# Two of the three sums of a woven weight slice, moved from VectorE to GpSimd

## The chip, the cores and the metric

The kernel runs on one core of a Trainium2 chip. The metric is the device time of one execution in microseconds (us). Before the change it is 2104.18 us, the median of 3 runs that lie between 2104.1 and 2104.22 us.

## The reference, cut to what matters

A two-layer decoder trunk over 256 tokens with 2048 columns, all in float32: layer 0 mixes by attention with a forget gate, layer 1 by dilated windows, and each mixer is followed by the same MLP, whose hidden width is 8192.

```
def sq_relu_mlp(h, w_up, w_down):
    a = jax.nn.relu(h @ w_up)
    return (a * a) @ w_down
...
    for i in range(DEPTH):
        ...
        x = x + mix.astype(x.dtype)
        h = rms_norm(x, mlp_norm_g[i])
        x = x + sq_relu_mlp(h, mlp_w_up[i], mlp_w_down[i]).astype(x.dtype)
```

The change touches only the product `h @ w_up` of the two MLPs, and of that only the part that is computed with seven half-size products.

## The kernel before, in words

**Weights in units.** All weights stream from HBM once, through five buffers `raw` of 128 x 2 x 512 floats. TensorE multiplies in a rounded float32 format, so each unit of weights is split in two: ScalarE copies the rounded part to `wh` (L376), and VectorE writes the rest, raw minus rounded, to `wl` (L382). There are five buffers each of `wh` and `wl`. A product needs three matmuls: rounded with rounded (L437), rounded with rest (L438), rest with rounded (L439). The split of a unit is issued when TensorE has used up the unit five places ahead of it, so at most four units lie ready ahead of TensorE.

**Plain units.** One plain unit feeds 12 matmuls of 512 columns, issued by `product_steps`.

**Woven slices.** Of each MLP's up-projection, 80 slices (10 column blocks, 8 slices each; 160 in the kernel) are computed with seven products of half the size in place of eight. They are woven between plain units of other products, at places that the tables `FIRST_BETWEEN`, `BETWEEN` and `LAST_BETWEEN` list; mostly one slice follows one plain unit. A slice takes up two units: the **quarters** unit, three quarters of the raw weights as they are (ScalarE's cast L370, VectorE's rest L374, both 768 wide), and the **sums** unit, four sums and differences of the raw quarters that are kept in a tile `quarters` (cast L376 from `quarters`, rest L382 from `quarters`). TensorE reads them in L1073 to L1077: nine matmuls on the quarters unit, twelve on the sums unit.

**The sums.** `sum_quarters` makes the sums in three instructions on VectorE: L394 (two differences at once, 512 columns), then L398 (256 columns, the tile's part `c`, from a raw quarter and a part that L394 wrote) and L400 (256 columns, `d`, from a raw quarter and `c`). It is a generator, so that the three stand at different places: L394 ahead of the plain unit's L382, L398 behind it, L400 ahead of the quarters unit's L374. There is one buffer `quarters`, shared with other work.

**What sets the order.** Each engine carries out its instructions in the order in which they were written; the function `pin` fixes that order. Small jobs of the MLP stand between the units: the seven products are combined by L1040 to L1048, which read PSUM, turned by L1005, and split by L1025 (ScalarE) and L1027 (VectorE).

**GpSimd.** Before the change it does little: 20 fills of a quarter with zeros (L368, at a block's first slice), a few powers (L598, L626), and it issues the 96 transfers that add a result to `x` in memory (L945), four at a time.

Of the kernel before, what the change touches and what calls it, by code (L numbers as in the profile page):

```python
# [21 lines left out]
NC = 512  # L22
# [21 lines left out]
HC = NC // 2  # L44
# [61 lines left out]
def trunk(ctx: ExitStack, tc, x, fox_w_in, fox_b_f, fox_q_gain, fox_k_gain, fox_w_out, dil_w_in,  # L106
          dil_q_gain, dil_k_gain, dil_w_out, mix_norm_g, mlp_norm_g, mlp_w_up, mlp_w_down, out):
    nc = tc.nc
# [250 lines left out]
    def split_part(i, part):  # L359
        nonlocal summing  # L360
        n, of = units[i]
        raw, (hi, lo) = raws[n], splits[i]
        if of == "sums":
            raw = quarters.pop()
        if "quarters" in of:

            if of == "first quarters":
                nc.gpsimd.memset(hi[:, 1, HC:NC].bitcast(F32), 0.0)  # L368
            flat_hi, flat_lo, flat = (x.rearrange("p k n -> p (k n)")[:, 0:3 * HC] for x in (hi, lo, raw))
            nc.scalar.copy(flat_hi, flat)  # L370
            for _ in summing or sum_quarters(n):
                pass
            summing = None
            nc.vector.tensor_sub(flat_lo, flat, flat_hi.bitcast(F32))  # L374
            return
        nc.scalar.copy(hi[:, part, :], raw[:, part, :])  # L376

        coming = i + 1 < len(units) and "quarters" in units[i + 1][1]
        if coming:
            summing = sum_quarters(units[i + 1][0])  # L380
            next(summing)
        nc.vector.tensor_sub(lo[:, part, :], raw[:, part, :], hi[:, part, :].bitcast(F32))  # L382
        if coming:
            next(summing)
# [3 lines left out]
    def sum_quarters(n):  # L388


        raw = raws[n]
        t = work.tile([P, 2, NC], F32, tag="sd", name=f"quarters{n}", bufs=1)
        neg, c, d = t[:, 0, HC:NC], t[:, 1, 0:HC], t[:, 1, HC:NC]
        nc.vector.tensor_sub(t[:, 0, :].rearrange("p (q n) -> p q n", q=2),  # L394
                             raw.rearrange("p k n -> p (k n)")[:, HC:3 * HC].rearrange("p (q n) -> p q n", q=2),
                             raw[:, 1, HC:NC].unsqueeze(1).to_broadcast([P, 2, HC]))
        yield
        nc.vector.tensor_add(c, raw[:, 0, HC:NC], neg)  # L398
        yield
        nc.vector.tensor_sub(d, raw[:, 0, 0:HC], c)  # L400
        quarters.append(t)

    def next_load():
# [842 lines left out]
```

## Time and profile before

| what | value |
|---|---|
| median of 3 runs | 2104.18 us (2104.1 to 2104.22) |
| span of the profiled execution | 2099.8 us |
| time outside the span (2104.18 less 2099.8) | 4.4 us |
| busy: TensorE matmul, VectorE, ScalarE, GpSimd | 2094.2, 1775.9, 1299.5, 141.3 us |
| granted TensorE clock | 1.00 throughout |
| woven stretches | 440 to 925 us and 1523 to 2022 us of the span |

The profile gives the span of one execution, from its first to its last instruction; its time as the runs measure it isn't given apart, so the 4.4 us between the span and the median are carried along unchanged. In the profile PE is TensorE, DVE VectorE, ACT ScalarE, POOL GpSimd, SP the queue that issues most DMAs. A row of the timeline has the start, the duration, the engine, the line, the operation, the tile written and those read, the shape, and in brackets the idle time before it with what ended it. A row of a group has the busy time, the mean of one in ns, and the idle time ahead. A row of the waits has the total, the number of times and the longest.

### The profile page before, as it was taken

To read this page: it belongs to the slowest core of one execution; us is meant where nothing else is said; L and a number is where in the kernel's file an instruction comes from. 1 tells how busy PE (TensorE), PEld (TensorE's weight loads), DVE (VectorE), ACT (ScalarE), POOL (GpSimd) and SP (SyncE) were. 2 spreads that over 40 slices of the span, in tenths; PEclk is the share of its full clock that TensorE was granted. 3 is DMA by queue.
4 is the path that set the end of the run, shared out by engine and by line. 5 is a ranking of instruction groups with operands and counts; after the bars stand their busy time and mean duration, and the time that the engine had idled before them with its cause. 6 is when DMAs were issued, how large, how long until landed. Compare 5 with 4: busy or idle time off the path is not lost.

```text
span 2099.8 us, 32579 instructions
## 1 busy us (share of the span) xinstructions
PE 2094.2 (100%) x11515; PEld 1881.5 (90%) x11515; DVE 1775.9 (85%) x2613; ACT 1299.5 (62%) x1895; POOL 141.3 (7%) x162
## 2 busy tenths in 40 slices
PE   9999999999999999999999999999999999999999
PEld 7888888899999999998888888888899999999998
DVE  6888876989999999998768787767899989999974
ACT  6565654766666666664655665646656766666663
POOL 2000000001100100110010010000001101001000
PEclk9999999999999999999999999999999999999999
DMA  8888877887888877887877776867878878788884
GB/s 258 254 264 262 259 248 222 272 261 241 252 243 249 262 240 252 258 249 236 280 239 230 247 242 211 269 202 243 277 231 261 241 250 248 231 251 256 265 262 152
DMA packets 375010, 518.28 MB, mean 247 GB/s; under 512 B 43112, under 2 KB 176576, under 8 KB 374848
## 3 DMA queue, kind: packets, MB, share of 16 engines
q1 hardware_dynamic: 360608, 503.23, 75.4%
q0 software_dynamic: 13824, 12.59, 4.0%
q8 instruction: 90, 1.47, 0.3%
q14 instruction: 72, 0.59, 0.1%
q10 hardware_dynamic: 416, 0.39, 0.1%
HBM read 463.12 MB, written 40.39 MB: 240 GB/s over the span
## 4 chain that ended last, share of the span: by engine, by line
PE 100%; DVE 0%; ACT 0%; issue 0%
PE acc L437 26%; PE acc L438 26%; PE acc L439 26%; PE halves_n L1077 6%; PE halves_n L1076 6%; PE halves_n L1075 6%; PE halves_n L1073 1%; PE sc_d L749 0%; PE sc_f L749 0%; PE po_f L698 0%; PE po_d L698 0%; PE sc_d L746 0%; PE acc L486 0%; PE acc L485 0%; PE acc L487 0%; PE pf L760 0%
## 5 line engine op out<-in xcount | busy, mean ns | idle before, releaser
L382 DVE TENSOR_TENSOR wl<-raw,wh 128x1024 fp32r<-128x1024 f32 (+1 forms) x643 | 775.6, 1214 | 228.0 <-ACT wh L376 217.9
L376 ACT CAST wh<-raw 128x1024 fp32r<-128x1024 f32 (+1 forms) x643 | 664.9, 1043 | 403.7 <-PE acc L439 323.7
L437 PE MATMUL acc<-wh,hT_n 128*128 128x512 f32 x1280 | 486.5, 380 | 0.4 <-ACT hT_n L580 0.3
L438 PE MATMUL acc<-wl,hT_n 128*128 128x512 f32 x1280 | 485.4, 379 | 0.0
L439 PE MATMUL acc<-wh,hT_n 128*128 128x512 f32 x1280 | 485.3, 379 | 0.0
L376 ACT CAST wh<-quarters 128x1024 fp32r<-128x1024 f32 x160 | 168.0, 1050 | 260.8 <-DVE quarters L400 243.4
L439 PEld LDWEIGHTS acc<-wh,hT_n 128*128 128x128 f32 x1280 | 241.9, 189 | 34.6 <-DVE hT_n L581 0.4
L437 PEld LDWEIGHTS acc<-wh,hT_n 128*128 128x128 f32 x1280 | 242.1, 189 | 33.2 <-ACT hT_n L580 1.0
L438 PEld LDWEIGHTS acc<-wl,hT_n 128*128 128x128 f32 x1280 | 242.2, 189 | 32.6 <-DVE wl L382 0.5
L382 DVE TENSOR_TENSOR wl<-quarters,wh 128x1024 fp32r<-128x1024 f32 x160 | 195.1, 1219 | 43.0 <-ACT wh L376 43.0
L437 PE MATMUL acc<-wh,aTh_n1a 128*128 128x512 f32 x512 | 194.3, 379 | 0.0
L438 PE MATMUL acc<-wl,aTh_n1a 128*128 128x512 f32 x512 | 194.0, 379 | 0.0
L439 PE MATMUL acc<-wh,aTl_n1a 128*128 128x512 f32 x512 | 194.0, 379 | 0.0
L438 PE MATMUL acc<-wl,aTh_n3a 128*128 128x512 f32 x480 | 182.2, 380 | 0.0
L437 PE MATMUL acc<-wh,aTh_n3a 128*128 128x512 f32 x480 | 182.1, 379 | 0.0
L439 PE MATMUL acc<-wh,aTl_n3a 128*128 128x512 f32 x480 | 181.9, 379 | 0.0
L1077 PE MATMUL halves_n<-wh,sums_n 128*128 128x256 f32 x640 | 176.0, 275 | 0.0
L1076 PE MATMUL halves_n<-wl,sums_n 128*128 128x256 f32 x640 | 176.0, 275 | 0.0
L1075 PE MATMUL halves_n<-wh,sums_n 128*128 128x256 f32 x620 | 170.5, 275 | 0.0
L374 DVE TENSOR_TENSOR wl<-raw,wh 128x768 fp32r<-128x768 f32 x160 | 152.3, 952 | 0.0
L370 ACT CAST wh<-raw 128x768 fp32r<-128x768 f32 x160 | 133.1, 832 | 28.9 <-PE acc L439 15.1
L1077 PE MATMUL halves_n<-wh,hT_n 128*128 128x256 f32 x480 | 132.0, 275 | 0.0
(660 smaller groups left out, 3499.1 us busy)
## 6 DMA issues: line engine op xcount, KB each, us to landing
raw<-in_mlp_w_up_dram SPq DMA_DIRECT2D x256, 512.0 KB, 5.1
raw<-in_mlp_w_down_dram SPq DMA_DIRECT2D x256, 512.0 KB, 4.9
raw<-in_dil_w_in_dram SPq DMA_DIRECT2D x192, 256.0 KB, 3.5
raw<-in_fox_w_in_dram SPq DMA_DIRECT2D x94, 512.0 KB, 4.8
raw<-in_fox_w_out_dram SPq DMA_DIRECT2D x32, 512.0 KB, 4.9
raw<-in_dil_w_in_dram SPq DMA_DIRECT2D x32, 512.0 KB, 4.4
raw<-in_dil_w_out_dram SPq DMA_DIRECT2D x32, 512.0 KB, 3.6
x<-y_n POOLq DMA_DIRECT2D x96, 128.0 KB, 6.0
```

The source lines that it names most:

```text
L370: nc.scalar.copy(flat_hi, flat)
L374: nc.vector.tensor_sub(flat_lo, flat, flat_hi.bitcast(F32))
L376: nc.scalar.copy(hi[:, part, :], raw[:, part, :])
L382: nc.vector.tensor_sub(lo[:, part, :], raw[:, part, :], hi[:, part, :].bitcast(F32))
L437: nc.tensor.matmul(acc[t], ah[:, tok], hi, start=first, stop=False)
L438: nc.tensor.matmul(acc[t], ah[:, tok], lo, start=False, stop=False)
L439: nc.tensor.matmul(acc[t], al[:, tok], hi, start=False, stop=last)
L1073: nc.tensor.matmul(banks[bank], ah, wide.rearrange("p b (h n) -> p b n h", h=2), start=True, stop=False)
L1075: nc.tensor.matmul(to, ah, hi, start=pr == 0 and i == 3, stop=False)
L1076: nc.tensor.matmul(to, ah, lo, start=False, stop=False)
L1077: nc.tensor.matmul(to, al, hi, start=False, stop=pr == KC // 2 - 1 and i > 2)
```

## The change

The two additions of 256 columns are issued on GpSimd. L394 stays on VectorE.

```
         yield
-        nc.vector.tensor_add(c, raw[:, 0, HC:NC], neg)
+        nc.gpsimd.tensor_add(c, raw[:, 0, HC:NC], neg)
         yield
-        nc.vector.tensor_sub(d, raw[:, 0, 0:HC], c)
+        nc.gpsimd.tensor_sub(d, raw[:, 0, 0:HC], c)
         quarters.append(t)
```

On VectorE, in a run of slices of the first MLP (the number behind a tile's name tells the tiles of one name apart; a row has line, operation, tile written, tiles read, shape):

```order
 L394 TENSOR_TENSOR quarters_4782<-raw_4670 128x512
 L382 TENSOR_TENSOR wl_4780<-raw_4640,wh_4779 128x1024
-L398 TENSOR_TENSOR quarters_4782<-raw_4670,quarters_4782 128x256
-L400 TENSOR_TENSOR quarters_4782<-raw_4670,quarters_4782 128x256
 L374 TENSOR_TENSOR wl_4801<-raw_4670,wh_4800 128x768
 L382 TENSOR_TENSOR wl_4818<-quarters_4782,wh_4817 128x1024
 L394 TENSOR_TENSOR quarters_4835<-raw_4731 128x512
```

The quarters unit's L374 now follows the plain unit's L382 directly, and nothing on VectorE stands between L374 and the sums unit's L382 in such a slice.

On GpSimd, a little further on in the same MLP, around one group of transfers and one fill:

```order
+L398 TENSOR_TENSOR quarters_5496<-raw_5380,quarters_5496 128x256
+L400 TENSOR_TENSOR quarters_5496<-raw_5380,quarters_5496 128x256
+L398 TENSOR_TENSOR quarters_5600<-raw_5535,quarters_5600 128x256
 L368 MEMSET wh_5618 128x256
+L400 TENSOR_TENSOR quarters_5600<-raw_5535,quarters_5600 128x256
```

The pairs stand in GpSimd's queue in the order of the slices; a block's first slice has the fill between its two additions.

And on GpSimd at the slice whose `quarters` tile has number 5823:

```order
+L398 TENSOR_TENSOR quarters_5823<-raw_5724,quarters_5823 128x256
 L945 DMA x_103<-y_n_2_0_0_220_5829 128x256
 L945 DMA x_103<-y_n_2_0_1_220_5832 128x256
 L945 DMA x_103<-y_n_2_1_0_220_5843 128x256
 L945 DMA x_103<-y_n_2_1_1_220_5846 128x256
+L400 TENSOR_TENSOR quarters_5823<-raw_5724,quarters_5823 128x256
```

Here four transfers stand between the slice's two additions; this is so at 4 of the 160 slices. L398 now waits for VectorE's L394, L400 for L398 on GpSimd, and ScalarE's cast of the sums for GpSimd. The order on TensorE and ScalarE is the same as before.

## The prediction

> **What bounds the kernel now.** I read the engines' busy times first, then what TensorE waited for.
>
> ```profile
> PE 2094.2 (100%) x11515; PEld 1881.5 (90%) x11515; DVE 1775.9 (85%) x2613; ACT 1299.5 (62%) x1895; POOL 141.3 (7%) x162
> ```
>
> ```profile
> PE spare L159 <- DVE zeros L155: 1.5, 1, 1.5
> PE acc L437 <- ACT hT_n L580: 0.3, 1, 0.3
> ```
>
> TensorE is busy for 2094.2 of 2099.8 us and waits 1.8 us in all, at the start. So nothing that makes VectorE faster can be worth more than those 1.8 us, under the 0.2% (4.2 us) that a measurement of this kernel can tell from no change. The question is only whether the change makes TensorE wait. So next the two woven stretches, the only places with L398 and L400 (columns: the stretch and its length, then busy time and instructions of PE, PEld, DVE, ACT, POOL):
>
> ```profile
> 440.00:925.00 485.00, 485.00 (x3017) 446.83 (x3017) 456.11 (x642) 319.28 (x438) 43.00 (x56) 1.00 0.82 248
> 1523.00:2022.00 499.00, 499.00 (x3103) 459.39 (x3102) 467.41 (x654) 327.18 (x447) 44.93 (x58) 1.00 0.82 249
> ```
>
> There VectorE is idle for only 485.0 - 456.1 = 28.9 and 499.0 - 467.4 = 31.6 us, 60.5 together. Most of this is one wait. From the list of waits, and from the view of the tile quarters (what its engines sat idle for, us and times):
>
> ```profile
> ACT wh L376 <- DVE quarters L400: 243.4, 129, 3.7
> ```
>
> ```profile
>   ACT wh L376: 43.0, 113
> ```
>
> In 129 of 160 slices ScalarE stands idle until L400 has ended. And VectorE's L382 on the sums waited for ScalarE's cast, 43.0 us in 113 slices. So in 113 slices the chain L394, L382, L398, L400, ScalarE's cast, L382 is unbroken, and VectorE's true slack is 60.5 - 43.0 = 17.5 us over 160 slices. One such slice on VectorE, and the cast:
>
> ```profile
> 865.73 0.69 DVE L394 TENSOR_TENSOR quarters<-raw 128x512 f32<-128x512 f32 x1
> 866.34 1.22 DVE L382 TENSOR_TENSOR wl<-raw,wh 128x1024 fp32r<-128x1024 f32 x1
> 867.47 0.42 DVE L398 TENSOR_TENSOR quarters<-raw,quarters 128x256 f32<-128x256 f32 x1
> 867.92 0.42 DVE L400 TENSOR_TENSOR quarters<-raw,quarters 128x256 f32<-128x256 f32 x1
> 868.27 0.95 DVE L374 TENSOR_TENSOR wl<-raw,wh 128x768 fp32r<-128x768 f32 x1
> 869.54 1.23 DVE L382 TENSOR_TENSOR wl<-quarters,wh 128x1024 fp32r<-128x1024 f32 x1 [0.32 <-ACT wh L376]
> 870.80 0.69 DVE L394 TENSOR_TENSOR quarters<-raw 128x512 f32<-128x512 f32 x1
> ```
>
> ```profile
> 868.46 1.05 ACT L376 CAST wh<-quarters 128x1024 fp32r<-128x1024 f32 x1 [2.34 <-DVE quarters L400]
> ```
>
> From L394 to the next L394 it is 870.80 - 865.73 = 5.07 us. TensorE's time for the same work, from one plain unit's first read of wl to the next one's, and its first read of this slice's sums:
>
> ```profile
> 869.26 0.38 PE L438 MATMUL acc<-wl,aTh_n1a 128*128 128x512 f32 x1
> 872.75 0.28 PE L1076 MATMUL halves_n<-wl,hT_n 128*128 128x256 f32 x1
> 874.20 0.38 PE L438 MATMUL acc<-wl,aTh_n1a 128*128 128x512 f32 x1
> ```
>
> 874.20 - 869.26 = 4.94 us. In a run of slices VectorE already needs 0.13 us more per slice than TensorE, and what it lies ahead is small: the sums' wl is done at 869.54 + 1.23 = 870.77 and read at 872.75, 1.98 us later. **Two engines are in balance here, and the reserve is about 2 us.** A delay of the chain L400 to L382 goes to TensorE almost at once.
>
> **The change part by part.** It takes 2 x 0.42 us per slice off VectorE. Alone that would be 0.84 x 160 = 134 us of VectorE's time, hidden behind TensorE, worth 0. What counts is when d, L400's result, is ready. All times now from the start of this slice's L394: before, L382 ends at 1.83 (867.56), L400 at 2.61 (868.34).
>
> Can GpSimd start L398 when L394 ends? These rows say no:
>
> ```profile
> 1057.02 1.23 DVE L382 TENSOR_TENSOR wl<-raw,wh 128x1024 fp32r<-128x1024 f32 x1
> 1078.62 1.23 DVE L382 TENSOR_TENSOR wl<-raw,wh 128x1024 fp32r<-128x1024 f32 x1 [0.85 <-DMA raw<-in_dil_w_in_dram]
> ```
>
> ```profile
> 1057.13 2.62 POOL L626 TENSOR_TENSOR rq_('dqk', 0, 0)_11300<-ss_('dqk', 0, 0)_11296,mhalf 128x8 f32<-128x8 f32 x1 [15.70 <-DVE ss_('dqk', 0, 0)_11296 L624]
> 1077.85 1.64 POOL L626 TENSOR_TENSOR rq_('dqk', 0, 1)_11484<-ss_('dqk', 0, 1)_11480,mhalf 128x8 f32<-128x8 f32 x1 [18.11 <-DVE ss_('dqk', 0, 1)_11480 L624]
> ```
>
> The same power of 8 columns takes 1.64 us while VectorE idles, and 2.62 us when it begins 0.11 us after an L382. It then ends at 1059.75, 1.50 us after that L382 (1058.25): it stood still until VectorE's instruction was over, and 0.14 us of its preparation was already done. L382 starts at 0.61, before L394 has ended at 0.69, so L398 will nearly always meet it. It waits until 1.83. The Trainium skill, SBUF — State Buffer, section "Who interferes with whom", states this as a rule: a VectorE instruction with two SBUF inputs and a GpSimd instruction that reads SBUF exclude each other, and the second blocks entirely. The rows agree for GpSimd as the second; no row here shows VectorE as the second.
>
> At 1.83 VectorE's next instruction, L374, is ready as well (its cast is long done; L398 before it began at once, at 1.74). It too reads two SBUF tiles. I take it that VectorE goes first, since its instructions follow each other with no gap: L374 runs from 1.74 to 2.69. Then VectorE has nothing until the cast of the sums, and GpSimd is alone.
>
> The price of one addition on GpSimd isn't in the trace. Nearest rows:
>
> ```profile
> 0.84 0.20 POOL masks.py:197 MEMSET ident<- 128x128 f32 x1
> 1.11 0.29 POOL masks.py:199 TENSOR_SCALAR_AFFINE_SELECT ident<-ident 128x128 f32<-128x128 f32 x1
> 1.36 0.10 POOL L150 MEMSET mhalf<- 128x8 f32 x1
> ```
>
> A near-empty fill takes 0.10 us; the select, with one input, (0.29 - 0.10) / 128 = 1.5 ns per column more. Two inputs read side by side would give 0.10 + 256 x 1.5 ns = 0.49 us, one after the other 0.88. I take the middle, 0.68. The gap between dependent instructions is 1.11 - 1.04 = 0.07 us. So d is ready at 2.69 + (0.68 - 0.14) + 0.07 + 0.68 = 3.98 instead of 2.61: **1.37 us later**. By 0.49 it is 3.60 (0.99 later), by 0.88 it is 4.38 (1.77). The Trainium skill, GPSIMD Engine Reference, section "Elementwise — side-by-side cycle accounting", gives 4497 ns for an addition of 2048 columns; in proportion, an estimate, 0.56 us, and the sum below would be about 2225.
>
> In the 113 unbroken slices cast and L382 come 1.37 us later, and the next slice's L394 with them: 113 x 1.37 = 155 us. In the other 47 VectorE has other work between. Where it reads PSUM (L1040 to L1048) the additions run beside it and the slice gets shorter; where it is a turn or a rest (L1005, L1027) the slice is still later, by less. I let these cancel: 0. At the upper price they add some 0.5 x 47 = 24.
>
> GpSimd's own queue: L398 and L400 now stand behind L945's transfers.
>
> ```profile
> 722.93 3.51 POOL L945 DMA_DIRECT2D x<-y_n  x4 [27.76 <-ACT y_n L944]
> ```
>
> Four take 3.51 us to issue, and they wait for ScalarE's y. Ahead of a slice's L398 they fall into time in which it would wait for VectorE anyway: 0. At the 4 slices where they stand between L398 and L400, up to 3.51 each: half, 7 us. The fill L368 has the same wait for TensorE as the quarters' cast: 0. The next raw transfer, which must wait for L400's read, is late by as much as the slice, and five buffers cover it: 0.
>
> What absorbs lateness: VectorE's slack of at most 17.5 us, of which I take half, 9, since part of it is waiting for transfers, and the reserve of 2 us at each stretch: 13 us.
>
> Sum: 155 + 0 + 7 - 13 = 149 us. The span becomes 2099.8 + 149 = 2249 and the time, with the 4.4 us outside, **2253 us**. By the low price 113 x 0.99 = 112, - 6 = 106: 2210. By the high 200 + 24 - 6 = 218: 2322.
>
> **The rivals.**
> *Alternation:* L398 gets its read at 1.83 and L374 has to wait for it, from 2.37 to 3.32, L400 behind that to 3.32 + 0.54 = 3.86: 1.25 later, 141 - 6 = 135, 2239 us. For it: L398 has waited longest; against: VectorE's instructions follow each other without a gap. The rule of SBUF — State Buffer in the Trainium skill, by which whichever starts first holds the other off, allows this order too.
> *Both additions ahead of L374:* L400 follows L398 before VectorE gets in. d is ready at 1.83 + 0.54 + 0.07 + 0.68 = 3.12, 0.51 later: 58 - 6 = 52, 2156 us. Against it: L400 is issued 0.07 us after L398, while L374 stands ready.
> *Not slower:* L398 isn't held up by L382. It runs from 0.69 + 0.09 = 0.78, d is ready at 0.78 + 0.68 + 0.07 + 0.68 = 2.21, ahead of the old 2.61; VectorE is relieved, TensorE has nothing to gain: 2104 us. It decides at an addition of 0.88 us. Against it stand the two L626 rows; for it, that a power reads 8 columns, and an addition may get its data otherwise.
> *A dearer addition:*
>
> ```profile
> 1040.71 0.72 POOL L598 TENSOR_TENSOR rstd_n<-ms_n,mhalf 128x2 f32<-128x2 f32 x1 [112.66 <-DVE ms_n L597]
> ```
>
> A power of 2 columns takes 0.72, of 8 columns 1.64: 0.15 per column and 0.41 fixed. If the 0.41 belongs to every GpSimd instruction with two inputs, an addition is 0.41 + 0.78 = 1.19 us, d is 2.39 later: 270 + 0.8 x 47 - 6 = 302, 2406 us. For it: same kind of instruction; against: the power's start-up is its own arithmetic.
>
> **How the numbers follow.** L374 first 0.38, alternation 0.25, both ahead 0.14, dearer 0.12, not slower 0.10, faster by some unforeseen way 0.01. The first two and the third reach from 2156 to 2322 with the price's bounds; I set 2150 to 2340, which leaves out no change, faster, and most of the dearer case: 2 in 10. Slower by over 0.2%: 0.38 + 0.25 + 0.14 + 0.12 = 0.89; within: 0.10; faster: 0.01.
>
> **What would show it.** L398 on GpSimd with a duration over 1 us, ending behind L382 or L374, and L400 near 0.7. ScalarE's wait of 243.4 us for L400 grown by over 100 us, now for GpSimd; VectorE's 43.0 us likewise, with VectorE's busy time down by some 134. TensorE's waits, 1.8 us now, near 150 us, on L438 and L1076 in the two stretches, and none outside. Wrong: L398 ending inside the L382, then "not slower"; L374 or L382 with longer durations of their own, then VectorE pays for the reads too; a TensorE clock under 1.00 in the stretches, which no row before shows.

## The result and the profile after

The changed kernel takes **2237.95 us** (median of 3 runs, 2237.81 to 2238.13) against 2104.18 us before: a ratio of 1.0639, 95% interval 1.0623 to 1.0654, 133.8 us more. The forecast was 2253 us in a range from 2150 to 2340; the rival "alternation" stood at 2239. The span of the profiled execution grew from 2099.8 to 2236.1 us, by 136.3. This execution took 2237.81 us in all, so 1.7 us lie outside its span and not the 4.4 that were carried along before the result; the runs of the kernel before that were made later have the same 1.7. The profile of the kernel before was thus of an execution some 2.7 us faster than the median of 2104.18, which is why span and time grew by slightly different amounts.

The engines' busy times after:

```profile
PE 2148.1 (96%) x11515; PEld 1900.2 (85%) x11515; DVE 1751.1 (78%) x2293; ACT 1289.1 (58%) x1895; POOL 587.2 (26%) x482
```

TensorE now idles for 2236.1 - 2148.1 = 88.0 us, 5.6 before: 82.4 more. Its busy time grew too, by 53.9 us for the same 11515 matmuls; the two make up the 136.3. A TensorE that is "96% busy" has lost 6% of its time here, because part of the waiting, and of a slower clock (below), is counted as busy: a matmul that starts 0.86 us after the one before it, where 0.11 is usual, is shown below with only 0.58 us of idle time. VectorE's busy time fell by only 24.8 us, not by the 134 us of the two additions that left it. Where TensorE idles, in the two stretches (columns: the stretch and its length, then busy time and instructions of PE, PEld, which is TensorE's loading of weights, DVE, ACT and POOL, then TensorE's clock, the share of DMA and its GB/s):

```profile
440.00:990.00 550.00, 510.04 (x3017) 454.66 (x3016) 442.80 (x484) 311.55 (x433) 258.48 (x210) 0.99 0.73 218
1590.00:2165.00 575.00, 533.67 (x3145) 475.55 (x3144) 461.13 (x503) 326.50 (x452) 268.66 (x218) 0.99 0.73 218
```

VectorE, the engine in balance with TensorE before, has slack as well now (107 of 550 us). No engine is busy all the time: they wait for each other. The list of waits says for what:

```profile
ACT wh L376 <- POOL quarters L400: 444.2, 146, 4.9
...
PEld halves_n L1076 <- DVE wl L382: 60.9, 80, 1.2
...
PE halves_n L1076 <- DVE wl L382: 45.5, 80, 1.0
...
PEld acc L438 <- DVE wl L382: 35.8, 64, 1.0
```

ScalarE's wait for L400 went from 243.4 us to 444.2, now for GpSimd; behind it TensorE waits for VectorE's wl. One slice in a run, up to the next slice's L394, on VectorE, GpSimd and ScalarE, and the matmul that waits for the wl of the sums:

```profile
523.10 0.69 DVE L394 TENSOR_TENSOR quarters<-raw 128x512 f32<-128x512 f32 x1
523.71 1.22 DVE L382 TENSOR_TENSOR wl<-raw,wh 128x1024 fp32r<-128x1024 f32 x1
524.84 1.48 DVE L374 TENSOR_TENSOR wl<-raw,wh 128x768 fp32r<-128x768 f32 x1
528.03 1.23 DVE L382 TENSOR_TENSOR wl<-quarters,wh 128x1024 fp32r<-128x1024 f32 x1 [1.71 <-ACT wh L376]
529.29 0.69 DVE L394 TENSOR_TENSOR quarters<-raw 128x512 f32<-128x512 f32 x1
```

```profile
523.92 1.58 POOL L398 TENSOR_TENSOR quarters<-raw,quarters 128x256 f32<-128x256 f32 x1 [3.19 <-ACT wh L370]
525.58 1.33 POOL L400 TENSOR_TENSOR quarters<-raw,quarters 128x256 f32<-128x256 f32 x1
```

```profile
526.95 1.06 ACT L376 CAST wh<-quarters 128x1024 fp32r<-128x1024 f32 x1 [3.46 <-POOL quarters L400]
```

```profile
528.46 0.28 PE L1075 MATMUL halves_n<-wh,hT_n 128*128 128x256 f32 x1
529.32 0.38 PE L1076 MATMUL halves_n<-wl,hT_n 128*128 128x256 f32 x1 [0.58 <-DVE wl L382]
```

Read it as three waits in turn (an instruction that stands still is shown as running: its duration is longer than it is elsewhere). L398 starts 0.13 us after L394's end (523.79), stands still until L382 is over (524.93), and ends 0.57 us later, at 525.50. L374 has started at 524.84 and lasts 1.48 us instead of 0.95: it stood still for 0.53 us, while L398 read. L400 has started at 525.58, stands still until L374 is over (526.32), and ends 0.59 us later, at 526.91. So L400's result is ready 3.81 us after L394's start, 2.61 before, and from L394 to the next one it is 6.19 us where it was 5.07. This is the rule: in 140 of the 160 slices L398 ends before L374 does and L400 after it.

All 160 slices, by group; L374 in the kernel before, then the changed kernel:

```profile
L374 DVE TENSOR_TENSOR wl<-raw,wh 128x768 fp32r<-128x768 f32 x160 | 152.3, 952 | 0.0
```

```profile
L374 DVE TENSOR_TENSOR wl<-raw,wh 128x768 fp32r<-128x768 f32 x160 | 230.3, 1440 | 1.0 <-ACT wh L370 0.9
L382 DVE TENSOR_TENSOR wl<-quarters,wh 128x1024 fp32r<-128x1024 f32 x160 | 195.9, 1224 | 218.9 <-ACT wh L376 218.9
...
L1027 DVE TENSOR_TENSOR aTl_n1a<-turned_n1a,aTh_n1a 128x512 fp32r<-128x512 f32 x32 | 27.7, 866 | 0.0
L1027 DVE TENSOR_TENSOR aTl_n3a<-turned_n3a,aTh_n3a 128x512 fp32r<-128x512 f32 x32 | 27.7, 866 | 0.0
```

```profile
L398 POOL TENSOR_TENSOR quarters<-raw,quarters 128x256 f32<-128x256 f32 x160 | 257.4, 1609 | 643.7 <-DVE quarters L394 257.4 <-ACT wh L370 241.1 <-ACT y_n L944 42.6
L400 POOL TENSOR_TENSOR quarters<-raw,quarters 128x256 f32<-128x256 f32 x160 | 205.4, 1284 | 10.7
```

L374 grew from 152.3 us in all to 230.3, L1027 from 43.9 to 55.4: VectorE pays 89.5 us of the 134 that it was spared. That leaves 45, and its busy time fell by 24.8, because neighbouring instructions overlap by some hundredths at their ends, which busy time counts once, and there is less of this overlap now. VectorE's wait for the cast of the sums rose from 43.0 to 218.9 us. On GpSimd an addition is shown with 1.6 or 1.3 us; the shortest of them took 0.73.

### The profile page after: what moved, and what is told of

Its sections match the earlier page's. It is cut to its first block, busy times and chain, and to the rows that moved or that the text cites. A ratio compares the mean times of both kernels' runs of the same rounds, so it can differ in the third digit from the quotient of the medians.

```text
span 2236.1 us, 32898 instructions
## 1 busy us (share of the span) xinstructions
PE 2148.1 (96%) x11515; PEld 1900.2 (85%) x11515; DVE 1751.1 (78%) x2293; ACT 1289.1 (58%) x1895; POOL 587.2 (26%) x482
## 3 DMA queue, kind: packets, MB, share of 16 engines
q8 instruction: 90, 1.47, 0.3%
## 5 line engine op out<-in xcount | busy, mean ns | idle before, releaser
L382 DVE TENSOR_TENSOR wl<-raw,wh 128x1024 fp32r<-128x1024 f32 (+1 forms) x643 | 774.5, 1213 | 218.7 <-ACT wh L376 212.9
L438 PE MATMUL acc<-wl,hT_n 128*128 128x512 f32 x1280 | 487.0, 380 | 3.2 <-DVE wl L382 2.9
L376 ACT CAST wh<-quarters 128x1024 fp32r<-128x1024 f32 x160 | 167.7, 1048 | 462.5 <-POOL quarters L400 444.2
L398 POOL TENSOR_TENSOR quarters<-raw,quarters 128x256 f32<-128x256 f32 x160 | 257.4, 1609 | 643.7 <-DVE quarters L394 257.4
L382 DVE TENSOR_TENSOR wl<-quarters,wh 128x1024 fp32r<-128x1024 f32 x160 | 195.9, 1224 | 218.9 <-ACT wh L376 218.9
L438 PEld LDWEIGHTS acc<-wl,hT_n 128*128 128x128 f32 x1280 | 242.7, 190 | 38.0 <-DVE wl L382 5.8
L374 DVE TENSOR_TENSOR wl<-raw,wh 128x768 fp32r<-128x768 f32 x160 | 230.3, 1440 | 1.0 <-ACT wh L370 0.9
L400 POOL TENSOR_TENSOR quarters<-raw,quarters 128x256 f32<-128x256 f32 x160 | 205.4, 1284 | 10.7
L438 PE MATMUL acc<-wl,aTh_n1a 128*128 128x512 f32 x512 | 197.6, 386 | 6.8 <-DVE wl L382 4.9
L438 PE MATMUL acc<-wl,aTh_n3a 128*128 128x512 f32 x480 | 185.7, 387 | 6.9 <-DVE wl L382 4.1
L1076 PE MATMUL halves_n<-wl,hT_n 128*128 128x256 f32 x480 | 141.4, 295 | 45.5 <-DVE wl L382 45.5
L1077 PE MATMUL halves_n<-wh,sums_n 128*128 128x256 f32 x640 | 178.4, 279 | 0.0
L1076 PE MATMUL halves_n<-wl,sums_n 128*128 128x256 f32 x640 | 178.2, 278 | 0.0
```

Of the source, the lines that this page charges most:

```text
L398: nc.gpsimd.tensor_add(c, raw[:, 0, HC:NC], neg)
L400: nc.gpsimd.tensor_sub(d, raw[:, 0, 0:HC], c)
L438: nc.tensor.matmul(acc[t], ah[:, tok], lo, start=False, stop=False)
L1076: nc.tensor.matmul(to, ah, lo, start=False, stop=False)
L1077: nc.tensor.matmul(to, al, hi, start=False, stop=pr == KC // 2 - 1 and i > 2)
```

## The experiments

Each kernel was timed against the kernel before on the same chip; from chip to chip that kernel's median lay between 2101.54 and 2104.18 us, so what follows are ratios, and differences to the kernel before on the same chip. The theory: a GpSimd addition and a VectorE instruction with two inputs in SBUF, the memory of the tiles, exclude each other, and what TensorE loses is the lateness of L400's result. Its rivals: the additions are simply slow on GpSimd, or handing over between engines is; VectorE's longer instructions are the loss; transfers in GpSimd's queue, or a part paid once, are. An edit that adds lines shifts the numbers of the lines behind it, so in some of the rows below L374, L382, L394, L398 and L400 have numbers a few higher; the order of the rows and the tiles tell which is which.

**1. Does the collision need two SBUF inputs?** In the changed kernel, L374 and the L382 behind L394 become an instruction with one input and the same length, a scaling that also keeps a running sum (`total`, a small tile).

```
-            nc.vector.tensor_sub(flat_lo, flat, flat_hi.bitcast(F32))
+            nc.vector.tensor_scalar(flat_lo, flat, 1e-4, 0.0, ALU.mult, ALU.add, accum_out=total)
...
-        nc.vector.tensor_sub(lo[:, part, :], raw[:, part, :], hi[:, part, :].bitcast(F32))
+        if coming:
+            nc.vector.tensor_scalar(lo..., raw..., 1e-4, 0.0, ALU.mult, ALU.add, accum_out=total)
+        else:
+            nc.vector.tensor_sub(lo[:, part, :], raw[:, part, :], hi[:, part, :].bitcast(F32))
```

> Both additions on GpSimd; the L382 behind L394 and L374 are replaced by a scaling of raw with a running sum, one SBUF input and about the same length, which leaves out the rests of those units. Collision theory, with two SBUF inputs as its condition: the additions take 0.73 us each and are ready at about 2.3 us, the scalings are not held up: 2100 to 2115 us. Slow-addition theory: L398 still 1.6 and L400 1.3 us: about 2238 us.

2102.32 us, ratio 0.9999 (0.9989 to 1.0008): nothing is lost. VectorE's two scalings and GpSimd's two additions of one slice:

```profile
512.04 1.21 DVE L385 TENSOR_SCALAR_CACHE_REDUCE wl<-raw 128x1024 fp32r<-128x1024 f32 x1
...
513.18 0.95 DVE L375 TENSOR_SCALAR_CACHE_REDUCE wl<-raw 128x768 fp32r<-128x768 f32 x1
```

```profile
512.25 0.74 POOL L404 TENSOR_TENSOR quarters<-raw,quarters 128x256 f32<-128x256 f32 x1 [3.20 <-DVE quarters L400]
513.07 0.73 POOL L406 TENSOR_TENSOR quarters<-raw,quarters 128x256 f32<-128x256 f32 x1
```

The additions run in the middle of the scalings, at 0.73 us each, and hold nobody up. GpSimd isn't slow in itself, and the hand-overs cost nothing that can be measured. The scalings also no longer wait for ScalarE's cast, but that can't be the reason: in the changed kernel VectorE idled ahead of these two instructions for 2 us in all.

**2. Each meeting by itself.** First only L374 gets one input, then only the L382 behind L394 (the same edits, one at a time).

> Both additions on GpSimd; only L374 is replaced by a scaling with one SBUF input (the rests of the quarters units are left out), the L382 behind L394 keeps its two. Collision theory: L398 waits for L382 and ends at 2.40 us, L400 runs at its free price and is ready at 3.2, nothing on VectorE is held up: about 0.6 us late per slice, 2155 to 2175 us. If only the meeting with L374 costs: 2100 to 2106 us.

2159.41 us, ratio 1.0266 (1.0249 to 1.0284), 56.2 us more than before. L398 still waits for L382, L400 in nearly all slices no longer for anything:

```profile
517.15 1.59 POOL L399 TENSOR_TENSOR quarters<-raw,quarters 128x256 f32<-128x256 f32 x1 [3.20 <-ACT wh L370]
518.82 0.73 POOL L401 TENSOR_TENSOR quarters<-raw,quarters 128x256 f32<-128x256 f32 x1
```

> Both additions on GpSimd; only the L382 behind L394 is replaced by a scaling with one SBUF input (the rests of those plain units are left out), L374 keeps its two. Collision theory: L398 takes 0.73 us from 0.8, L400 has its read before L374 begins and is ready at 2.4, ahead of 2.61, while L374 waits and takes about 1.4 us: 2100 to 2108 us. If the meeting with L374 alone is enough to cost: 2150 us or more.

2102.83 us, ratio 0.9998 (0.9989 to 1.0008). Here L400 and L374 meet the other way round:

```profile
518.75 1.44 DVE L374 TENSOR_TENSOR wl<-raw,wh 128x768 fp32r<-128x768 f32 x1
```

```profile
518.64 0.73 POOL L405 TENSOR_TENSOR quarters<-raw,quarters 128x256 f32<-128x256 f32 x1
```

```profile
L374 DVE TENSOR_TENSOR wl<-raw,wh 128x768 fp32r<-128x768 f32 x160 | 203.9, 1275 | 8.1 <-ACT wh L370 8.1
```

The addition, first by 0.11 us, takes its free 0.73, and L374 stands still for 0.49. L374 is over 1.2 us long in 102 of the 160 slices (in 148 in the changed kernel), 51.6 us longer in all than before, and nothing is lost. So a longer L374 alone isn't what costs: against the VectorE-time rival. The loss begins with the wait for L382, which makes L400's result late. The two meetings don't add up, 56.2 and 0 against 133.8: with both additions on GpSimd, only a late L398 lets L374 start ahead of L400, and L400 then waits for it as well.

**3. One addition at a time.** First, against the changed kernel, L398 stays on GpSimd and L400 goes back to VectorE.

```
         nc.gpsimd.tensor_add(c, raw[:, 0, HC:NC], neg)
...
-        nc.gpsimd.tensor_sub(d, raw[:, 0, 0:HC], c)
+        nc.vector.tensor_sub(d, raw[:, 0, 0:HC], c)
```

> L398 stays on GpSimd, L400 goes back to VectorE. Collision theory (an addition on GpSimd and a VectorE instruction with two SBUF inputs exclude each other, and what counts is when L400's result is ready): L398 ends 0.57 us after L382, at 2.40 us from L394's start, L400 on VectorE at about 2.85 instead of 2.61, L374 back at 0.95 us; 113 x 0.24 to 0.32, less the reserve: 2120 to 2140 us. VectorE-time theory (the cost is that L374 and L1027 last longer): L374 is not held up any more, so about 2104 us.

2118.26 us, ratio 1.0079 (1.0062 to 1.0095), 16.7 more; L400's result is ready 2.87 us after L394's start (median of the slices), 0.25 later than before. The time lies 1.7 us below the expected range, less than the 2.6 us by which the kernel before was faster on this chip. With L398 on VectorE and L400 on GpSimd instead:

> L398 goes back to VectorE, L400 stays on GpSimd. Collision theory: L400 is asked for at 2.25 us, while L374 has run since 2.08, so it waits for its end at 3.03 and is ready at 3.60 instead of 2.61 us; L374 at 0.95 us; 113 x 0.99 less 6 = 106: 2200 to 2220 us. VectorE-time theory: L374 is not held up, so about 2104 us.

2202.02 us, ratio 1.0477 (1.0462 to 1.0493), 100.5 more, ready at 3.61. Both are near what the theory gave; where VectorE's time would decide, neither should have cost anything, since L374 takes 0.95 us in both (in the second one in 152 of 160 slices), and VectorE was busy for some 50 us less than before. The second kernel shows who goes first:

```profile
521.99 0.95 DVE L374 TENSOR_TENSOR wl<-raw,wh 128x768 fp32r<-128x768 f32 x1
```

```profile
522.21 1.33 POOL L400 TENSOR_TENSOR quarters<-raw,quarters 128x256 f32<-128x256 f32 x1 [4.68 <-issue]
```

L374 began 0.22 us ahead, so here it is L400 that stands still. In all these rows the one that started first goes through undisturbed.

**4. The order.** One more instruction on VectorE, ahead of L374, which reads L400's result, so that L374 can't come between the additions:

```
+            seen = small.tile([P, 1], F32, tag="seen", name=f"seen{i}")
+            nc.vector.tensor_copy(seen, quarters[-1][:, 1, HC:HC + 1])
             nc.vector.tensor_sub(flat_lo, flat, flat_hi.bitcast(F32))
```

> Both additions on GpSimd, and a copy of one column of L400's result ahead of L374 on VectorE, so that L374 can't come between the two. Collision theory: L398 ends at 2.40, L400 follows at its free price of 0.73 and is ready at 3.20 instead of 3.81 us; 0.6 us late per slice against the kernel before: 2155 to 2180 us. Slow-addition theory (GpSimd needs 1.6 and 1.3 us for its additions whatever VectorE does, plus the hand-overs): L400 still at 3.8 and L374 behind it: 2238 us or more.

2185.63 us, ratio 1.0402 (1.0387 to 1.0418), 84.1 more. L400's result is ready at 3.22, as expected (the additions L398 and L400 stand in L400 and L402 here):

```profile
526.30 1.59 POOL L400 TENSOR_TENSOR quarters<-raw,quarters 128x256 f32<-128x256 f32 x1 [3.20 <-DVE quarters L396]
527.96 0.73 POOL L402 TENSOR_TENSOR quarters<-raw,quarters 128x256 f32<-128x256 f32 x1
```

Taking L374 out of the middle gives back 50 us of 134, but the time lies 6 us above the expected range. From the rows of all slices, from L394's start to the last L382's end against the kernel before: the 98 slices with no other work on VectorE in between became 0.62 us longer on average, where the changed kernel has 1.17; the 46 with a turn or another rest in between became 0.58 longer, hardly less than the 0.65 in the changed kernel. I take the reason to be that VectorE can't do that work while it waits ahead of L374; no run shows this by itself.

**5. What does lateness cost without GpSimd?** The kernel before, with L398 and L400 each issued twice on VectorE.

> The kernel before with L398 and L400 each issued twice on VectorE, nothing on GpSimd: 0.84 us more per slice. If a late chain goes to TensorE at once because VectorE and TensorE are in balance: 160 x 0.84 = 134 less the reserve of 13, about 2225 us (2210 to 2235). If the trouble is GpSimd's own and VectorE's reserve covers such an amount: 2104 to 2120 us.

2227.67 us, ratio 1.06 (1.0584 to 1.0616), 126.1 more. VectorE and TensorE were in balance: 134 us more on VectorE cost nearly that much. But here VectorE has more to do and L400's result is late too, by 0.92 us (median), so this run can't tell the two apart. The runs in which VectorE had less to do can: L400's result 0.25, 0.60 and 1.00 us later (the first of experiment 3, the first of experiment 2, the second of experiment 3) went with 16.7, 56.2 and 100.5 us, and 1.20 in the changed kernel with 133.8. Experiment 4 lost more for the same 0.60, 84.1 us; there L374 is late as well.

**6. Fills in place of the additions.**

```
-        nc.gpsimd.tensor_add(c, raw[:, 0, HC:NC], neg)
+        nc.gpsimd.memset(t[:, 1, :], 0.0)
...
-        nc.gpsimd.tensor_sub(d, raw[:, 0, 0:HC], c)
+        nc.gpsimd.memset(t[:, 1, :], 0.0)
```

> The two additions are replaced by fills with zeros on GpSimd, each over the 512 columns of both sums, which leaves the two sums out. A fill reads nothing. Collision theory: the fills take about 0.52 us each, don't wait for L382 and don't hold up L374 (0.95 us); the second is ready at about 1.95 us, ahead of 2.61: 2100 to 2106 us, although VectorE is relieved of 134 us. Hand-over theory (the two crossings between the engines cost, whatever is done there): well over 2104, up to 2238 us.

2101.72 us, ratio 0.9998 (0.9988 to 1.0007). A fill takes 0.53 us (median), also beside L382, and TensorE waits for nothing in the stretches; its only wait is at the start:

```profile
512.89 0.53 POOL L400 MEMSET quarters<- 128x512 f32 x1
```

```profile
512.90 1.22 DVE L382 TENSOR_TENSOR wl<-raw,wh 128x1024 fp32r<-128x1024 f32 x1
```

```profile
PE spare L159 <- DVE zeros L155: 1.5, 1, 1.5
```

VectorE is free of the additions in this kernel, and the kernel is no faster for it: the 134 us were never worth anything.

**7. Half the slices.** Only the slices of the first MLP, those ahead of `MIDDLE`, have both additions on GpSimd.

```
+        on = nc.gpsimd if n < MIDDLE else nc.vector
```

> The additions on GpSimd in the first MLP only, 80 of the 160 slices. If each slice pays for itself: half of 134, about 2171 us (2165 to 2177). If one part is paid once, or the second stretch pays for lateness of the first: away from the half, under 2160 or over 2180 us.

2169.73 us, ratio 1.0325 (1.0309 to 1.034), 67.7 more: half of 133.8. Each stretch pays for its own slices, and no part is paid once.

**8. The transfers in GpSimd's queue.** L400 goes to VectorE at the slices with L945 between the additions (156 additions L400 stay on GpSimd).

> As the changed kernel, but at slices where transfers (L945) stand between the two additions in GpSimd's queue, L400 goes to VectorE. If those four slices cost up to 3.5 us each and lower TensorE's clock after them: 10 to 25 us less, 2213 to 2228 us. If the transfers fall into time in which L400 waits anyway: 2238 us.

2223.95 us, ratio 1.0578 (1.0563 to 1.0594), 121.9 more, so about 12 us of the 133.8 belong to these four slices, a difference of two measurements that are each good to some 3 us. One of the slices in the changed kernel, and TensorE there:

```profile
573.53 1.59 POOL L398 TENSOR_TENSOR quarters<-raw,quarters 128x256 f32<-128x256 f32 x1 [3.20 <-ACT y_n L944]
575.06 3.50 POOL L945 DMA_DIRECT2D x<-y_n  x4
577.28 2.02 POOL L400 TENSOR_TENSOR quarters<-raw,quarters 128x256 f32<-128x256 f32 x1
```

```profile
580.44 0.48 PE L1075 MATMUL halves_n<-wh,hT_n 128*128 128x256 f32 x1 [1.98 <-ACT wh L376]
```

L400 ends at 579.30, 0.74 us after the last transfer was issued (578.56), and TensorE stands idle for 1.98 us until the cast behind it is done. In these four slices L400's result is ready 6.6 us after L394's start, 2.8 later than in the others: 11 us for the four. The 12 us include what the slices lose without transfers too.

## Why the prediction came out right, point by point

**The bound.** That VectorE's relief is worth 0 is shown by the fills (ratio 0.9998). That lateness of the chain goes to TensorE is shown by L400 alone on GpSimd: 1.00 us late, VectorE busy for some 50 us less, 100.5 us lost.

**L398 waits for L382.** Right, and shown by experiment 2: without that wait nothing is lost.

**"I take it that VectorE goes first" failed.** L374 and L398 were both ready when L382 ended, and L398, which had waited, got its read; L374 stood still for 0.53 us, and then L400 for L374. This is the rival "alternation": 3.86 forecast, 3.81 measured, against 3.98 of the main case. The two orders lie only 14 us apart in time, 2239 and 2253, so that 2253 came so near says nothing for the order that I took. The reason that I gave, that VectorE's instructions follow each other with no gap, wasn't one. The Trainium skill, SBUF — State Buffer, section "Who interferes with whom", has the rule that whichever starts first blocks the other; L374 at 1.44 behind an addition and at 0.95 ahead of one (experiments 2 and 3) agree with it in both directions, and the fills agree that a GpSimd instruction that only writes isn't concerned.

**The price of an addition.** 0.68 taken, 0.73 measured where it was free, within the bounds (at the 1.47 ns per column of the two rows these are 0.48 and 0.86, not 0.49 and 0.88, which changes nothing). In the Trainium skill's GPSIMD Engine Reference the section "Elementwise — side-by-side cycle accounting" led to the estimate of 0.56, below what the runs show for this size.

**113 x 1.37 = 155, and 0 for the other 47, failed as a split.** From the rows of all slices, from L394's start to the last L382's end: 98 slices with nothing else between became 1.17 us longer on average (115 us), 46 with a turn or a rest between 0.65 (30 us), and 16 with PSUM work 0.17 (3 us), together 148. The 40 us that the first term had too many and the 33 that the second lacked nearly cancelled, which was luck. The slices with PSUM work did not get shorter on the whole.

**The queue and the reserve.** 7 us for the four slices with transfers, 11 by the rows, L400's result being 2.8 us late in each. 13 us for what absorbs lateness: 148 by the slices less the 136.3 of the span is about 12. The 4.4 us outside the span were 1.7.

**The signs.** L398 above 1 us, ScalarE's wait up by 201 us and VectorE's wait for the cast up by 176 came as said. L400 was to be near 0.7 and has 1.33 (median), because it waits for L374. TensorE's waits lie in the two stretches as said, but 88 us of idle time are not the 150 that were forecast: the rest shows as busy time; and besides L438 and L1076 the list has waits of 14 us for VectorE's L1045, which reads PSUM, and of 6 for ScalarE's cast. Two signs of being wrong came too. L374 has longer durations and VectorE's busy time fell by 24.8 and not by 134, so VectorE pays as well, but experiment 2 shows that this payment alone isn't what the time is lost on. And the clock fell below 1.00 in the stretches (last section).

## What to carry to other kernels

An engine that is 7% busy isn't free help for one that is 85% busy when both read SBUF: look up, for each place, what the busy engine does while the other is to read, and whose instruction starts first. Before a move for an engine's load, see in the list of waits whether the bound engine waits for that engine at all; here it didn't, and the moved work lay on the chain with 2 us of reserve. If such work must move, put it where the other engine works with one SBUF input (experiment 1) or partly from PSUM (an L400 of the changed kernel took its 0.73 us at 506.61 beside L1047 and L1048), or see that GpSimd starts first: in experiment 2 0.11 us were enough.

## What the runs showed of the hardware that wasn't expected

TensorE's clock fell to half for 3.4 or 6.8 us at a time, at five places and 23.9 us in all, in the changed kernel; before it was full throughout. The stretches around one of these places, with the columns as above:

```profile
577.20:580.60 3.40, 1.42 (x12) 1.20 (x10) 0.18 (x1) 1.26 (x2) 2.11 (x3) 1.00 1.17 223
580.60:584.00 3.40, 2.62 (x12) 2.33 (x12) 3.37 (x4) 1.99 (x3) 1.50 (x1) 0.50 0.47 162
584.00:587.40 3.40, 3.40 (x10) 2.77 (x10) 1.71 (x2) 1.87 (x2) 1.41 (x2) 0.50 0.72 166
```

In the 3.4 us ahead of it TensorE was busy for 1.42, with one wait of about 2 us in it, the one behind the four transfers; the first row of the clock column still has 1.00, the next two 0.50. The Trainium skill, TensorE: Matmul & The Clock Gate, section "HAM oscillation — how this bites in real kernels", puts the limit at gaps of over about 3.4 us; here a window that was idle for more than half was enough, with no single gap above 1.99 us. The five falls begin at 580.58, 734.18, 1730.88, 1962.98 and 2058.55, whole multiples of 3.413 us apart, and in the 3.41 us ahead of each TensorE was busy for 1.27 to 1.51; of the other such windows at full clock, the first 20 us and the last 10 left aside, one had 1.50 and kept the full clock, all others 2.09 or more. The doubled additions, with nothing on GpSimd, have four such falls as well, so they don't need GpSimd.

How much of the 133.8 us the clock cost wasn't measured apart: at most 12 us, half of the 23.9, and less where TensorE waits for wl anyway and a slower matmul costs nothing.
